# A batched float32 matrix product on one core: moving the transposes of the last three batches from the batch before into their own batch

## The chip, the cores and the metric

The kernel runs on one core of a Trainium2 chip. The metric is device time in microseconds (us) of one execution. Medians of several executions are given. Two numbers must be kept apart: the device time of a run, and the span of its profile, which goes from the first to the last instruction of the kernel and is 1.7 to 1.9 us shorter. Profiles show one execution each, so times that are read inside a profile are compared with an anchor inside the same profile.

## The reference

```python
def setup_inputs():
    batch, m, k, n = 32, 512, 1024, 768
    # x: [32, 512, 1024] float32, weight: [32, 1024, 768] float32, random normal

def reference(x, weight):
    return np.matmul(x, weight).astype(np.float32)
```

## The kernel before

Each batch loads x (2 MiB of float32 in HBM, the chip's main memory) and the weight (3 MiB), both cast to bfloat16 on the way by GpSimd's DMA queue, and stores 1.5 MiB of float32. (Only x of batch 0 is loaded otherwise: by SP, as float32.) TensorE (PE) must have x transposed, so it also does transposes: four of them make one row tile `xT` of 128 rows, which VectorE copies out of PSUM, the memory that PE writes to. A batch has four row tiles `mt`; two of them make a pair, whose results are copied out by ScalarE and VectorE (`evacuate`).

The last four batches (`CHUNKED`) take their weight in pieces along the contraction, so that PE can start before the whole weight is there. All other loads and the stores of outputs 0 to 30 are issued by GpSimd; the two halves of output 31 are issued by SP (SyncE), on another DMA queue.

```python
    CHUNKED = {B - 4: (4, 4), B - 3: (4, 4), B - 2: (4, 4), B - 1: (4, 2, 2)}
    AHEAD = 3
    # ... (pools, loads)
    def transpose(b, mt):
        pt = tpsum.tile([P, JT, P], F32, name="pt")
        pairs = xs[b].bitcast(F32)
        for j in range(JT):
            nc.tensor.transpose(pt[:, j, :], pairs[:, mt, j::JT], ident)
        xT = xT_pool.tile([P, JT, P, 2], BF16, name="xT")
        nc.vector.tensor_copy(...)          # cut
        return xT
    # ... (first batch, matmuls)
    def evacuate(b, pair, pm):
        o = outs[b][:, pair * N2:(pair + 1) * N2]
        nc.scalar.copy(o[:, 0:512], pm[0])
        nc.vector.tensor_copy(o[:, 512:1024], pm[1])
        nc.scalar.copy(o[:, 1024:N2], pm[2])
    # ...
        ready = {}
        for b in range(B):
            if b + AHEAD < B:
                load_x(b + AHEAD)
                load_w(b + AHEAD)
            if b > 0:
                nc.gpsimd.dma_start(out=out_view[b - 1], in_=outs[b - 1])
            outs[b] = out_pool.tile([P, MT * N], F32, name="out_sb")
            if b not in CHUNKED:
                # ... (cut: batches 0 to 27, untouched by the change)
                continue
            xT = ready.pop(b, None) or {mt: transpose(b, mt) for mt in range(MT)}
            pms = [banks() for _ in range(2)]
            at = 0
            for n in CHUNKED[b]:
                last = at + n == KT
                for mt in range(MT):
                    if last and b + 1 < B:
                        ready.setdefault(b + 1, {})[mt] = transpose(b + 1, mt)
                    matmuls(pms[mt // 2], mt % 2, xT[mt], b, range(at, at + n), True)
                    if last and mt % 2 == 1:
                        pair = mt // 2
                        evacuate(b, pair, pms[pair])
                        if b == B - 1:
                            cols = slice(pair * N2, (pair + 1) * N2)
                            nc.sync.dma_start(out_view[b, :, cols], outs[b][:, cols])
                at += n
```

## Time and profile before

| | before |
|---|---|
| device time, median of 3 | 516.92 us (516.58 to 517.77) |
| span of the profile | 516.0 us |
| PE / VectorE / ScalarE busy | 83% / 25% / 15% |
| x 31 landed, last half of output 31 landed | 489.1 us, 514.8 us |

From the page of the kernel before: the DMA queue table (packets, MB, share of the sixteen DMA engines' span) and the summary of the chain of waits by engine.

```profile
q0 software_dynamic: 14256, 131.60, 98.9%
q1 hardware_dynamic: 432, 3.67, 1.9%
...
DMA 88%; PE 9%; issue 1%; DVE 0%; ACT 0%; POOLq 0%
```

Queue 0 (GpSimd's) keeps the sixteen DMA engines busy for 98.9% of the span, and the chain of waits is nearly all DMA. The kernel is bound by DMA, at a fixed beat: 1.5 MiB (counted as float32) land every 3.66 us.

The timeline of the kernel before, some lines of its tail (start, duration, engine, line, operation, and in brackets the idle time before it and what ended it):

```profile
479.18 6.66 PE L99 MATMUL pm<-w_sb,xT 128*128 128x256 bf16 x39
...
489.12 0.75 PE L68 MATMUL pt<-ident,x_sb 128*128 128x128 f32 x4 [3.28 <-DMA x_sb<-in_x_dram]
...
496.67 11.86 PE L99 MATMUL pm<-w_sb,xT 128*128 128x256 bf16 x71
...
499.19 0.53 POOL L130 DMA_DIRECT2D out_dram<-out_sb  x1 [16.95 <-ACT out_sb L112]
...
507.89 1.62 SPq L159 DMA_DIRECT2D out_dram<-out_sb  x2
```

PE stops at about 485.8 us and waits for x 31, with half of batch 30 still to do, because the transposes of 31 stand before that half. So output 30 is issued by GpSimd only at 499.19, and output 31 by SP at 507.89 (and 509.2).

How long those stores took, from the list of DMA issues in the tail of the kernel before (KB each, median us from issue to landing):

```profile
out_dram<-out_sb POOLq DMA_DIRECT2D x1, 1536.0 KB, 11.9
out_dram<-out_sb SPq DMA_DIRECT2D x2, 768.0 KB, 5.3
```

Output 30 landed at 499.19 + 11.9 = 511.1 us. Issue plus time to landing gives every landing in this text; below they are given to a hundredth, from the semaphore events of the trace.

The DMA engines over the tail of the kernel before, in stretches of 2 us (the last two columns are the busy share of the sixteen engines and GB/s):

```profile
core 0: us, PE busy (x) PEld busy (x) DVE busy (x) ACT busy (x) POOL busy (x), PEclk, DMA share, GB/s
503.00:505.00 2.00, 1.95 (x13) 1.13 (x12) 0.00 (x0) 0.00 (x0) 0.00 (x0) 1.00 0.97 412
505.00:507.00 2.00, 2.00 (x14) 1.27 (x13) 0.00 (x0) 0.44 (x1) 0.00 (x0) 1.00 0.75 320
507.00:509.00 2.00, 1.53 (x10) 0.68 (x7) 1.33 (x2) 1.70 (x4) 0.00 (x0) 1.00 0.45 187
509.00:511.00 2.00, 0.00 (x0) 0.00 (x0) 0.05 (x1) 0.16 (x1) 0.00 (x0) 1.00 1.01 415
511.00:513.00 2.00, 0.00 (x0) 0.00 (x0) 0.00 (x0) 0.00 (x0) 0.00 (x0) 1.00 0.80 326
```

The dip at 505 to 509 us looks like time that an earlier output 31 could fill.

### The profile page before, as it was taken

What the parts mean: (1) busy time and instruction counts of PE and PEld (TensorE: products, weight loads), DVE (VectorE), ACT (ScalarE), POOL (GpSimd) and SP (SyncE); (2) the same over time, 40 slices, a digit from 0 to 9 for tenths busy, and PEclk for the clock granted to TensorE, in tenths of its full rate; (3) what the DMA queues carried; (4) which work ended last, traced back from release to release, by engine and by line L of the source; (5) the groups of instructions that cost most, each with busy time, mean ns of one, the idle gap of its engine ahead of it and who ended that gap; (6) DMA issues with size and microseconds to landing.
All of it is one profiled execution on the core that took longest, in us unless ns stands there. A gap on an engine that the chain in (4) does not pass through costs nothing.

```text
span 516.0 us, 5924 instructions
## 1 busy us (share of the span) xinstructions
PE 426.4 (83%) x2528; PEld 279.6 (54%) x2576; DVE 129.7 (25%) x196; ACT 76.3 (15%) x129; POOL 53.4 (10%) x105
## 2 busy tenths in 40 slices
PE   0999998698887879977798797987878987969794
PEld 0766665465554555654555464654545554646462
DVE  0433333133131231322313232222223132312221
ACT  0111111011111111110111011111111110101111
POOL 3011010100101001100011001010100110111000
PEclk9999999799898997998989799898989898979989
DMA  8999999999999999999999999999999999999996
GB/s 255 218 218 211 215 274 275 272 272 241 255 280 273 275 254 241 276 277 274 267 240 268 274 276 272 247 252 278 275 274 256 247 267 275 276 267 239 259 390 261
DMA packets 14714, 135.65 MB, mean 263 GB/s; under 512 B 1632, under 2 KB 1632, under 8 KB 3040
## 3 DMA queue, kind: packets, MB, share of 16 engines
q0 software_dynamic: 14256, 131.60, 98.9%
q1 hardware_dynamic: 432, 3.67, 1.9%
q8 instruction: 20, 0.33, 0.2%
q14 instruction: 6, 0.05, 0.0%
HBM read 167.77 MB, written 50.33 MB: 423 GB/s over the span
## 4 chain that ended last, share of the span: by engine, by line
DMA 88%; PE 9%; issue 1%; DVE 0%; ACT 0%; POOLq 0%
DMA x_sb<-in_x_dram 37%; DMA w_sb<-in_weight_dram 25%; DMA out_dram<-out_sb 24%; PE pm L99 7%; DMA x_first<-in_x_dram 2%; PE pt L81 1%; PE pt L68 1%; DVE out_sb L111 0%; DVE xT L70 0%; ACT out_sb L112 0%; POOLq L130 0%; POOLq L54 0%; POOLq L60 0%
## 5 line engine op out<-in xcount | busy, mean ns | idle before, releaser
L99 PE MATMUL pm<-w_sb,xT 128*128 128x256 bf16 (+1 forms) x2000 | 370.2, 340 | 60.9 <-DMA w_sb<-in_weight_dram 56.8
L99 PEld LDWEIGHTS <-xT 128*128 128x128 bf16 x2048 | 206.8, 102 | 198.3 <-issue 66.5
L70 DVE COPY xT<-pt 128x1024 bf16<-128x1024 bf16 x124 | 83.0, 689 | 245.4 <-PE pt L68 245.4
L68 PE MATMUL pt<-ident,x_sb 128*128 128x128 f32 x496 | 77.4, 290 | 8.9 <-DMA x_sb<-in_x_dram 8.6
L68 PEld LDWEIGHTS pt<-ident,x_sb 128*128 128x128 f32 x496 | 73.7, 207 | 17.2 <-issue 7.1
L110 ACT COPY out_sb<-pm 128x512 f32<-128x512 f32 x64 | 37.5, 586 | 289.6 <-PE pm L99 280.7
L111 DVE COPY out_sb<-pm 128x512 f32<-128x512 f32 x64 | 43.9, 687 | 115.5 <-PE pm L99 114.8
L112 ACT COPY out_sb<-pm 128x512 f32<-128x512 f32 x64 | 37.5, 586 | 142.5 <-PE pm L99 142.4
L54 POOL DMA_DIRECT2D x_sb<-in_x_dram x31 | 16.5, 533 | 172.8 <-DMA w_sb<-in_weight_dram 141.6
L60 POOL DMA_DIRECT2D w_sb<-in_weight_dram x37 | 19.8, 534 | 132.4 <-DMA out_dram<-out_sb 65.6
L130 POOL DMA_DIRECT2D out_dram<-out_sb x31 | 16.6, 536 | 140.8 <-DMA x_sb<-in_x_dram 62.8
L81 PE MATMUL pt<-ident,x_first 128*128 128x128 f32 x32 | 5.7, 338 | 12.4 <-DMA x_first<-in_x_dram 12.4
L81 PEld LDWEIGHTS pt<-ident,x_first 128*128 128x128 f32 x32 | 4.9, 202 | 13.0 <-issue 12.3
L82 DVE CAST xT<-pt 128x512 bf16<-128x512 f32 x8 | 5.5, 727 | 18.4 <-PE pt L81 18.3
L110 ACT ACT_TABLE_LOAD x1 | 1.3, 1283 | 0.7 <-PEq L175 0.7
masks.py:199 POOL TENSOR_SCALAR_AFFINE_SELECT ident<-ident 128x128 f32<-128x128 f32 x1 | 0.3, 288 | 0.1
masks.py:197 POOL MEMSET ident<- 128x128 f32 x1 | 0.2, 223 | 0.0
L175 POOL MEMSET const-float32-0.0<- 128x1 f32 x1 | 0.1, 99 | 0.2 <-issue 0.2
L175 POOL MEMSET const-bfloat16-1.0<- 128x1 bf16 x1 | 0.1, 102 | 0.0
L175 POOL MEMSET const-uint8-127<- 128x1 uint8 x1 | 0.1, 102 | 0.0
L175 POOL MEMSET const-float32-1.0<- 128x1 f32 x1 | 0.1, 98 | 0.0
## 6 DMA issues: line engine op xcount, KB each, us to landing
out_dram<-out_sb POOLq DMA_DIRECT2D x31, 1536.0 KB, 41.9
w_sb<-in_weight_dram POOLq DMA_DIRECT2D x28, 1536.0 KB, 43.2
x_sb<-in_x_dram POOLq DMA_DIRECT2D x31, 1024.0 KB, 39.6
w_sb<-in_weight_dram POOLq DMA_DIRECT2D x7, 768.0 KB, 32.5
x_first<-in_x_dram SPq DMA_DIRECT2D x1, 2048.0 KB, 11.5
out_dram<-out_sb SPq DMA_DIRECT2D x2, 768.0 KB, 5.3
w_sb<-in_weight_dram POOLq DMA_DIRECT2D x2, 384.0 KB, 28.7
```

Source lines behind the costliest of these rows:

```text
L54: nc.gpsimd.dma_start(out=xs[b], in_=x_view[b])
L60: nc.gpsimd.dma_start(out=ws[b][:, at:at + n, :], in_=w_view[b, :, at:at + n, :])
L68: nc.tensor.transpose(pt[:, j, :], pairs[:, mt, j::JT], ident)
L70: nc.vector.tensor_copy(xT.rearrange("p j m r -> p (j m r)"), pt.bitcast(BF16).rearrange("p j m -> p (j m)"))
L81: nc.tensor.transpose(pt[:, i, :], x_first[:, mt, JT * h + i::KT], ident)
L82: nc.vector.tensor_copy(xT[:, 2 * h:2 * h + 2].rearrange("p j m r -> p j r m"), pt.rearrange("p (j r) m -> p j r m", r=2),)
L99: nc.tensor.matmul(pm[bank][:, at:at + size], xT[:, ko // 2, :, ko % 2], ws[b][:, ko, off:off + size], start=(ko == 0 and not (together an ...
L110: nc.scalar.copy(o[:, 0:512], pm[0])
L111: nc.vector.tensor_copy(o[:, 512:1024], pm[1])
L112: nc.scalar.copy(o[:, 1024:N2], pm[2])
L130: nc.gpsimd.dma_start(out=out_view[b - 1], in_=outs[b - 1])
L175: nc = _bacc.Bacc("TRN2", target_bir_lowering=False, num_devices=1)
```

## The change

The intent: a batch's transposes should not stand in the way of the batch before. In the last four batches they are issued in the batch's own first chunk, each one tile ahead of its matmuls. (Batch 28 did its own transposes before the change too, all four ahead of its matmuls; for batches 29 to 31 they move.) Nothing is added or removed; only PE's order changes.

```diff
-        ready = {}
         for b in range(B):
@@
-            xT = ready.pop(b, None) or {mt: transpose(b, mt) for mt in range(MT)}
+            xT = {0: transpose(b, 0)}
@@
                 for mt in range(MT):
-                    if last and b + 1 < B:
-                        ready.setdefault(b + 1, {})[mt] = transpose(b + 1, mt)
+                    if mt + 1 not in xT and mt + 1 < MT:
+                        xT[mt + 1] = transpose(b, mt + 1)
                     matmuls(pms[mt // 2], mt % 2, xT[mt], b, range(at, at + n), True)
```

## The prediction

> **What bounds the kernel.** The DMA. The queue table gives queue 0 (GpSimd's) 98.9% of the sixteen engines' span; the chain of waits is 88% DMA, 9% PE. Landings (issue plus time to landing) come at a fixed beat: 1.5 MiB of float32 per 3.66 us (an output, or half a weight, counted at float32), 4.86 us for the 2 MiB of an x. That is 430 GB/s; the Trainium skill ("DMA: Bandwidth & Descriptors", Specifications) gives 435 GB/s as the fabric ceiling, and this trace sits on it. 208 MiB at that beat take 507.5 us of the 516.0 us span (estimate).
>
> **What the change does.** Nothing is added or removed: transposes, matmuls, copies, DMAs and the order of GpSimd's issues stay. Only PE's order in the last four batches changes. Before, the second half of batch b stood behind the transposes of b+1, so behind x of b+1: the timeline shows PE restarting at 457.5, 473.3 and 489.1 us, when x 29, 30 and 31 land, with half of the batch before still to do. After, batch b needs only its own x and w.
>
> Costs: four transposes about 0.65 us, their copy 0.69 us, half a batch of matmuls 5.1 to 5.4 us warm. With w halves landing at 461.0/464.7, 476.9/480.6 and, for batch 31, 492.7/494.6/496.5, I estimate PE's end of batch 29 at 470 instead of 479, of 30 at 486 instead of 497, of 31 at 504 to 506 instead of 508.6. Batch 31 keeps a cold start (granted clock 0.57 in 490 to 494 before): PE idles before x 31 and before w 31. Output 30 is then issued about 487 instead of 499.2, output 31 from 504 instead of 507.9.
>
> **How much is critical.** Nearly nothing. The tail looks like a loss: the DMA share falls to 0.60, 0.43, 0.46 in 506 to 509 us, 1.6 us missing. But landings show no gap: outputs 27 to 30 at 500.1, 503.8, 507.5, 511.1, the halves of 31 at 513.0 and 514.8, all on the beat (1.85 for a half). I read this as sixteen engines finishing their backlogs unevenly: the fast ones run dry at 505.5 us, the slowest works without pause to the end. An output has landed when its slowest engine is done, so output 31 queued earlier fills only idle engines. Both queues share the same engines (same page, "Issuing engines are not separate DMA queues"); the slowest has the same bytes to move. Output 30 was already queued 8 us before its turn, the second half of 31 about 2 us.
>
> **Predicted time:** 516.8 us, 516.0 to 517.8 (three runs before spread over 1.2 us). Faster by over 2%: 0.005; within 2%: 0.99; slower: 0.005.
>
> **What would show each step.** Right: PE no longer waits for x 29, 30, 31 with old work behind it; last matmul at 503 to 507 us; output 31 issued some 3 us earlier; more DMA share in 505 to 509, less in 509 to 513; yet the last landing near 514.8, x 31 near 489, same beat. Wrong: a last landing near 513, so the dip was a true loss.
>
> **What would make it wrong.** The slowest engine did wait for output 31 (at most 1.6 us: 515.2). Or w 31 or the cold clock push the last matmul past 510 (about +1). Or interleaving the queues longer changes its beat. Stray pauses of 0.5 to 1 us (landings at 250.9, 445.2) come and go and are as large as any effect here.

## More of the kernel before

The next lines were there before the prediction too, but I did not look at them. They are instructions of the kernel's closing sequence, which all stand under one line (L186, `with _tile.TileContext(nc) as tc:`): the view of that source line gives the count, the shortest, median and longest duration in ns, and the start of the first and the last.

```profile
L186 POOLq EVENT_SEMAPHORE  x4: 17/17/17, 515.2 to 515.9; - x4
L186 POOLq DRAIN  x3: 46/102/16031, 499.2 to 515.7; - x3
L186 SPq DRAIN  x3: 7/7/7, 514.9 to 515.5; - x3
```

GpSimd's DRAIN begins at 499.17 us, together with its issue of output 30 (499.19), and this one instruction takes 16.03 us: it ends at 515.20 us. SP, which waits for the last landing (514.80), is through at 514.94. So the end of the program waited for GpSimd's drain, by 0.26 us, and not for the last landing.

## The result, and the profile after

| | before | after |
|---|---|---|
| device time, median (range), 6 runs each | 516.88 us (516.58 to 517.77) | 518.25 us (517.45 to 519.31) |
| ratio | | 1.0025 (95%: 1.0011 to 1.0039) |

A ratio is the mean time of one kernel's fast runs over that of the other's of the same rounds, so it is not quite the ratio of the medians. The change costs about 1.3 us. That is within 2%, but outside noise and outside the predicted range (516.0 to 517.8).

The profile of after has a span of 517.5 us. The same timeline lines, of after:

```profile
482.39 7.96 PE L99 MATMUL pm<-w_sb,xT 128*128 128x512 bf16 x48
...
490.19 1.12 PE L68 MATMUL pt<-ident,x_sb 128*128 128x128 f32 x8
...
491.41 0.53 POOL L129 DMA_DIRECT2D out_dram<-out_sb  x1 [9.33 <-ACT out_sb L112]
...
498.48 7.96 PE L99 MATMUL pm<-w_sb,xT 128*128 128x512 bf16 x48
...
505.80 1.62 SPq L158 DMA_DIRECT2D out_dram<-out_sb  x2
```

PE did what was intended: batch 30 is finished before PE turns to x 31, output 30 is issued 7.8 us earlier and output 31 2.1 us earlier. The stores of after, from its list of DMA issues:

```profile
out_dram<-out_sb POOLq DMA_DIRECT2D x1, 1536.0 KB, 21.3
out_dram<-out_sb SPq DMA_DIRECT2D x2, 768.0 KB, 7.8
```

Output 30, though issued earlier, landed later: 491.41 + 21.3 = 512.7 us. The DMA engines over the tail of after:

```profile
core 0: us, PE busy (x) PEld busy (x) DVE busy (x) ACT busy (x) POOL busy (x), PEclk, DMA share, GB/s
503.00:505.00 2.00, 2.00 (x15) 1.22 (x14) 0.00 (x0) 0.54 (x1) 0.00 (x0) 1.00 1.01 430
505.00:507.00 2.00, 1.44 (x9) 0.67 (x7) 1.38 (x2) 1.70 (x4) 0.00 (x0) 1.00 0.86 363
507.00:509.00 2.00, 0.00 (x0) 0.00 (x0) 0.00 (x0) 0.06 (x1) 0.00 (x0) 1.00 1.00 418
509.00:511.00 2.00, 0.00 (x0) 0.00 (x0) 0.00 (x0) 0.00 (x0) 0.00 (x0) 1.00 0.89 372
511.00:513.00 2.00, 0.00 (x0) 0.00 (x0) 0.00 (x0) 0.00 (x0) 0.00 (x0) 0.53 0.49 206
```

The dip is filled, and the bytes are missing later. The closing sequence of after (its line is L185):

```profile
L185 POOLq EVENT_SEMAPHORE  x4: 17/17/17, 516.8 to 517.4; - x4
L185 POOLq DRAIN  x3: 46/102/25367, 491.4 to 517.2; - x3
L185 SPq DRAIN  x3: 7/7/7, 515.3 to 517.0; - x3
```

GpSimd's drain starts at 491.39, takes 25.37 us and ends at 516.76. SP had been through at 515.36 and waited 1.4 us for it. Set beside the landings, the two profiles agree to a hundredth:

| us | before | after |
|---|---|---|
| x 31 landed | 489.08 | 489.49 |
| output 29 landed | 507.45 | 507.87 |
| output 30 landed | 511.11 | 512.67 |
| last half of output 31 landed | 514.80 | 515.22 |
| ... counted from x 31 | 25.72 | 25.73 |
| GpSimd's drain ended | 515.20 | 516.76 |
| ... counted from output 30's landing | 4.09 | 4.09 |
| end of span, counted from the drain's end | 0.76 | 0.76 |

Of the 1.56 us between the two spans, 0.41 us were already there when x 31 landed (it landed between 487.9 and 489.5 us in the thirteen traces, whatever the kernel), and the rest, 1.15 us, is the later landing of output 30.

### The profile page after: what moved, and what is told of

Its sections match the earlier page's. It is cut to its first block, busy times and chain, and to the rows that moved or that the text cites. A ratio compares the mean times of both kernels' runs of the same rounds, so it can differ in the third digit from the quotient of the medians.

```text
span 517.5 us, 5978 instructions
## 1 busy us (share of the span) xinstructions
PE 428.0 (83%) x2576; PEld 278.9 (54%) x2576; DVE 129.8 (25%) x196; ACT 76.2 (15%) x129; POOL 53.3 (10%) x105
## 4 chain that ended last, share of the span: by engine, by line
DMA 81%; PE 15%; issue 1%; DVE 1%; ACT 0%; POOLq 0%
DMA w_sb<-in_weight_dram 47%; DMA out_dram<-out_sb 25%; PE pm L99 12%; DMA x_sb<-in_x_dram 8%; DMA x_first<-in_x_dram 2%; PE pt L68 1%; PE pt L81 1%; DVE xT L70 1%; DVE out_sb L111 0%; ACT out_sb L112 0%; POOLq L60 0%; POOLq L54 0%
## 5 line engine op out<-in xcount | busy, mean ns | idle before, releaser
L68 PE MATMUL pt<-ident,x_sb 128*128 128x128 f32 x496 | 75.5, 286 | 1.1 <-DMA x_sb<-in_x_dram 1.1
## 6 DMA issues: line engine op xcount, KB each, us to landing
w_sb<-in_weight_dram POOLq DMA_DIRECT2D x2, 384.0 KB, 28.7
```

## The theories

**Tail theory.** The end of the program waits for GpSimd's closing drain, and the drain ends 4.09 us after GpSimd's own last store, output 30, has landed. Output 31 is on the other queue. Queued earlier, its packets take turns with those of output 30 on the slowest DMA engine; the sum of bytes is the same, so the last landing does not move, but output 30 lands later, and with it the end of the drain. The Trainium skill ("DMA: Bandwidth & Descriptors", section "Queues, rings and completion order") says that each DMA engine goes round the queue rows that have work for it, a packet at a time. The sizes of the delays in these traces agree with that (below, under the table of all tails).

**Rivals.** PE: its new order, its idle times or its clock cost the time (in the profile of after the granted clock, the share of its full clock that PE was given, was 0.57 in 494 to 498 us). Noise: the 0.41 us and their like, pauses in the DMA beat that come and go.

## The experiments

Runs of one group were on the same chip and share the runs of the kernel before.

### First group: the changed kernel again, its halves, and a needless delay

**after_again**: the changed kernel, no edit.

> The changed kernel as it is, once more, for a second trace and a closer interval. Tail theory (GpSimd's last drain returns about 4.1 us after its last own store, output 30, has landed, and output 31, queued earlier on the other DMA queue, takes turns with output 30 on the slowest DMA engine): 1.0 to 1.6 us slower than before; output 30 lands 1.0 to 1.4 us later than 3.66 us after output 29; the drain ends 4.1 us after that landing; output 31 still lands 25.7 us after x 31. Rival, noise and stray pauses early in the run: within 0.4 us of before, or slower with x 31 landing later by as much. Rival, PE: the last matmul would be later than before's 508.5 us.

Measured: 518.39 us against 517.01, ratio 1.0025 (1.0013 to 1.0037). In its trace output 31 was issued at 502.7, even earlier: this time PE had the full clock in batch 31 (granted 1.00 from 486 to 498 us; last matmul at 503.3). It had the low one before, in batch 30 (0.61 and 0.54 in 474 to 482 us). Output 30 landed 5.50 us after output 29, so 1.84 us late, and the drain ended 4.09 us after that. The last landing came 25.76 us after x 31. The delay of output 30 was larger than the 1.0 to 1.4 us expected. The rest held. So the loss is repeatable, it is there without a cold clock in batch 31 (and in only31_own, below, with a clock of 1.00 in every stretch from 470 to 502 us), and it is there with PE ending 4 us earlier than in the kernel before (503.3 against 507.4 in before_again below, whose x 31 landed at the same 488.0 us).

**only31_own** and **own_but31**: half of the change each. A set `OWN` names the batches that transpose for themselves; the others are served a batch ahead as before. It holds `(B - 1,)` in the first and `(B - 4, B - 3, B - 2)` in the second.

```diff
-            xT = ready.pop(b, None) or {mt: transpose(b, mt) for mt in range(MT)}
+            xT = {0: transpose(b, 0)} if b in OWN else ready.pop(b, None) or {mt: transpose(b, mt) for mt in range(MT)}
@@
-                    if last and b + 1 < B:
+                    if mt + 1 not in xT and mt + 1 < MT:
+                        xT[mt + 1] = transpose(b, mt + 1)
+                    if last and b + 1 < B and b + 1 not in OWN:
```

> Only batch 31 is changed: its transposes are among its own matmuls; 29 and 30 are still transposed a batch ahead. Tail theory: all of the loss is here, 1.0 to 1.6 us slower than before, output 31 issued near 506 and 507 us, output 30 late by over 0.8 us against the beat. Rival, that the loss comes from PE's idle times and cold clock in all of the batches 28 to 31: a part of it, about a third.

> The complement: batches 28 to 30 are changed, 31 is still transposed a batch ahead, among the last matmuls of 30. Tail theory: level with before within 0.4 us, since output 31 is issued near 508 and 509 us as before and output 30 lands on the beat. Rival, that the loss comes from PE's idle times and cold clock in the batches 28 to 31: about two thirds of the loss, 0.8 us slower than before.

Measured: batch 31 alone 518.50 us, ratio 1.0028 (1.0016 to 1.0041); batches 28 to 30 alone 517.00 us, ratio 0.9999 (0.9987 to 1.0011), both against 517.01. The whole loss comes with batch 31 and none with the other three. Output 31 was issued at 502.9 us in the first (expected: near 506) and at 507.0 in the second. The drains, from the view of the closing line of each kernel, first of batch 31 alone:

```profile
L189 POOLq DRAIN  x3: 46/93/24967, 491.2 to 516.7; - x3
```

and of batches 28 to 30 alone:

```profile
L189 POOLq DRAIN  x3: 46/93/16022, 498.2 to 514.8; - x3
```

The first ends at 491.24 + 24.97 = 516.21 us, the second at 498.25 + 16.02 = 514.27 us. Output 30 was 1.83 us late against the beat in the first and 0.03 us in the second.

**after_late_store**: the changed kernel, with four needless copies on ScalarE that hold output 31 back. The result is the same.

```diff
                     if last and mt % 2 == 1:
                         pair = mt // 2
+                        if b == B - 1 and pair == 0:
+                            for _ in range(4):
+                                nc.scalar.copy(outs[b][:, 0:512], pms[0][0])
                         evacuate(b, pair, pms[pair])
```

> The changed kernel with four needless copies of the first PSUM bank on ScalarE ahead of the last batch's copies, so that both stores of output 31 are issued about 2.3 us later, where the kernel before has them. Same result, same values. Tail theory: output 30 lands on the beat again (3.66 to 4.0 us after output 29), the drain ends earlier, and the kernel is 0.8 to 1.4 us faster than the changed kernel, level with before within 0.4 us, although its last store is issued later. Any rival in which the end waits for the last store or for PE: no faster than the changed kernel, up to 2 us slower.

Measured: 517.27 us, ratio 1.0000 (0.9987 to 1.0012) against before, 1.1 us faster than the changed kernel of the same rounds (518.39). Added work and a later last store (504.8 and 505.8 us, against 502.7 and 504.0 in after_again, the trace of the same rounds) made the kernel faster. This is what the tail theory says and what no theory allows in which the end waits for PE or for the last store. One number was off: output 31 was issued at 504.8 us, still 1.5 us before output 29 had landed, so output 30 was 0.67 us late, not on the beat.

### Second group: which queue the last stores are on

**before_pool_store** and **after_pool_store**: output 31 is issued by GpSimd, behind output 30 in the same queue. One edit, made in both kernels:

```diff
-                            nc.sync.dma_start(out_view[b, :, cols], outs[b][:, cols])
+                            nc.gpsimd.dma_start(out_view[b, :, cols], outs[b][:, cols])
```

> The kernel before with the two stores of output 31 issued by GpSimd, not by SP, so that they stand in GpSimd's own queue behind output 30. Tail theory: output 31 lands at about the same time after x 31 (25.7 us, up to 0.5 more), the drain ends 4.1 us after that, so the span ends about 4.9 us after the last landing and not 1.2: 3 to 4.5 us slower than before. Rival (the end follows the last landing whatever the queue): within 0.7 us of before.

> The changed kernel with the same edit. With one queue there are no turns to take: outputs 30 and 31 land on the beat, one after the other. Tail theory: 3 to 4.5 us slower than before, and level with the kernel before that has the same edit, within 0.5 us; the loss by the change is gone, although PE's order differs as before. Rival, that PE's order costs the time: again 1.0 to 1.6 us slower than the kernel before with this edit.

Measured: 521.12 us and 520.69 us against 517.09, both with ratio 1.0074 (1.0062 to 1.0086). The loss by the change is gone once there is only one queue, although PE's order still differs (last matmul at 507.8 and at 503.6 us). Output 30 landed 3.71 and 3.65 us after output 29, on the beat, even with output 31 queued at 503.4. And both pay about 3.8 us, because now the drain follows the last store of all. The drain of the kernel before with this edit:

```profile
L186 POOLq DRAIN  x3: 46/87/9450, 508.8 to 518.8; - x3
```

It ends at 508.85 + 9.45 = 518.30 us, 4.17 us after the last half of output 31 (514.13). In the changed kernel with this edit it ends 4.17 us after the same landing as well (514.02, 518.19).

**before_sp30** and **after_sp30**: output 30 is taken from GpSimd and issued by SP between the two halves of output 31. Again one edit in both:

```diff
-            if b > 0:
+            if 0 < b < B - 1:
                 nc.gpsimd.dma_start(out=out_view[b - 1], in_=outs[b - 1])
@@
                             nc.sync.dma_start(out_view[b, :, cols], outs[b][:, cols])
+                            if pair == 0:
+                                nc.sync.dma_start(out_view[b - 1], outs[b - 1])
```

> The kernel before with output 30 taken from GpSimd's queue and issued by SP between the two halves of output 31. GpSimd's last store is output 29, so its drain ends near 511.6 us and off the critical path; the end follows the last landing by about 1.2 us. But the slowest DMA engine has nothing left from about 505.7 us until output 31 is issued at 507.9[...]. Tail theory: that engine idles for 2.5 to 3 us, and the kernel is 2 to 3 us slower than before. Rival, that the last landing does not depend on PE's end: level with before.

> The changed kernel with the same edit. Output 31's first half is issued at 505.8 us, just when the slowest engine runs dry. Tail theory: GpSimd's drain ends near 512 us, the slowest engine pauses for no more than 0.6 us, the span ends about 1.2 us after the last landing: 0.6 to 1.4 us faster than the changed kernel, within 0.5 us of before, and 2 to 3 us faster than the kernel before with this edit; here PE's earlier end is worth what it saves. Rival, that the loss is PE's: still 1.0 to 1.6 us slower than before.

Measured, against 517.09: the kernel before with this edit 518.19 us, ratio 1.0015 (1.0000 to 1.0029), with a wide spread (516.74 to 519.34); the changed kernel with this edit 516.42 us, ratio 0.9988 (0.9976 to 1.0000). Now the changed kernel is the faster one of the pair, by 1.8 us of the medians (about 1.4 us by the two ratios). That is less than the 2 to 3 us expected.

The drain is off the critical path in both: it ends at 510.57 and 510.40 us, 4.05 us after output 29. What decides is whether the DMA engines run dry before output 31 comes. The kernel before with this edit:

```profile
core 0: us, PE busy (x) PEld busy (x) DVE busy (x) ACT busy (x) POOL busy (x), PEclk, DMA share, GB/s
503.00:505.00 2.00, 2.00 (x14) 1.18 (x13) 0.00 (x0) 0.00 (x0) 0.00 (x0) 1.00 0.36 154
505.00:507.00 2.00, 2.00 (x15) 1.26 (x13) 0.69 (x1) 1.23 (x3) 0.00 (x0) 1.00 0.06 25
507.00:509.00 2.00, 0.62 (x4) 0.12 (x2) 0.69 (x1) 1.07 (x2) 0.00 (x0) 1.00 0.60 246
```

and the changed kernel with this edit:

```profile
core 0: us, PE busy (x) PEld busy (x) DVE busy (x) ACT busy (x) POOL busy (x), PEclk, DMA share, GB/s
503.00:505.00 2.00, 0.26 (x2) 0.00 (x0) 0.69 (x1) 0.71 (x2) 0.00 (x0) 1.00 0.89 372
505.00:507.00 2.00, 0.00 (x0) 0.00 (x0) 0.00 (x0) 0.00 (x0) 0.00 (x0) 0.84 1.09 458
507.00:509.00 2.00, 0.00 (x0) 0.00 (x0) 0.00 (x0) 0.00 (x0) 0.00 (x0) 0.50 0.96 406
```

Where the engines ran dry, the last landing came 27.68 us after x 31; where they did not, 25.78. In the seven traces of the table below it was 25.72 to 25.77, so the slowest engine had not paused in them, as the prediction read it. The pause cost 1.9 us of landing, less than the 2.5 to 3 us expected, and 1.1 us of the median, less than the 2 to 3 us expected.

### Third group: noise, and a version for the end

**before_again**: the kernel before against itself.

> The kernel before against itself, for a second trace of it and for the size of the noise. Ratio 1.000 within 0.0015. GpSimd's drain ends 4.09 us after output 30 has landed, the span 0.75 us after the drain; output 30 lands within 0.1 us of the 3.66 us beat after output 29.

Measured: 517.50 us against 516.99, ratio 1.0006 (0.9994 to 1.0018). The drain ended 4.09 us after output 30, which landed exactly on the beat. So a ratio of 1.0006 between runs of one kernel is noise, and 1.0025 twice is not.

**after_sp30_again**: no further edit.

> The changed kernel with output 30 issued by SP between the halves of output 31, once more, for a closer interval against before. 0.3 to 1.2 us faster than before (ratio 0.998 to 0.9995); the span ends 0.9 us after the last landing, which comes 25.8 us after x 31.

Measured: 516.69 us against 516.99, ratio 0.9995 (0.9982 to 1.0008). With the first time (0.9988), this version is 0.3 to 0.7 us of the medians below the kernel before, but the second interval includes no difference. It beats the changed kernel clearly, and the kernel before at best by a hair.

**after_sp30_k15**: a gamble on the slowest DMA engine.

```diff
-                            nc.sync.dma_start(out_view[b, :, cols], outs[b][:, cols])
+                            for rows in (slice(0, 120), slice(120, P)):
+                                nc.sync.dma_start(out_view[b, rows, cols], outs[b][rows, cols])
```

(and the same for output 30).

> The same, with the three stores of SP each cut into 120 and 8 partitions, a gamble on which DMA engine is the slowest. If a store of 120 partitions goes to fifteen of the engines and the one it leaves out is the slowest, the last landing comes 1 us earlier after x 31 (about 24.7 us) and the kernel is about 1 us faster than the uncut one. If another engine is the slowest, that one gets more to do: 0.2 to 0.8 us slower than the uncut one.

Measured: 521.05 us, ratio 1.0087 (1.0066 to 1.0109), 4.4 us slower than the uncut version of the same rounds. In its tail the DMA share was 0.95, 0.96 and 0.99 in the three stretches of 2 us from 505 to 511, which does not tell whether the cut left an engine out. The last landing came 28.7 us after x 31, 3 us later than uncut. The gamble is lost, by more than either branch of the expectation allowed, and it does not tell which engine is the slowest.

### All tails side by side

"Lead" is how long before output 29's landing SP issued the first half of output 31. "Late" is how much output 30's landing missed the beat of 3.66 us after output 29.

| kernel | lead | output 30 late | last landing from x 31 | end of span from x 31 | median |
|---|---|---|---|---|---|
| before | -0.44 | 0.00 | 25.72 | 26.88 | 516.88 |
| before_again | -0.40 | 0.00 | 25.77 | 26.92 | 517.50 |
| own_but31 | -0.48 | 0.03 | 25.75 | 26.92 | 517.00 |
| after_late_store | 1.48 | 0.67 | 25.77 | 27.60 | 517.27 |
| after | 2.07 | 1.14 | 25.73 | 28.03 | 518.25 |
| after_again | 3.69 | 1.84 | 25.76 | 28.76 | 518.39 |
| only31_own | 3.71 | 1.83 | 25.75 | 28.73 | 518.50 |

The landing of the last half (fourth column) is constant. The end of the span (fifth) grows with the lateness of output 30 (third), one for one. The lateness is about half of the lead (second) in the four traces that have one.

The list of DMA packets in the packed traces tests the turn-taking more closely. GpSimd's queue moves output 30 in 128 packets of 12,288 bytes; SP's moves each half of output 31 in 128 packets of 6,144. If both are spread evenly over the sixteen engines (not shown), an engine has 8 packets of each, and one of SP's takes about 0.23 us (an estimate: the second half lands 1.83 us after the first in the kernel before). The delays 0.67, 1.14 and 1.84 us are then nearly whole numbers of SP's packets, 3, 5 and 8: as if one went in between for each packet of output 30 that was still to come. The turns do not begin with the issue, though: SP's first packet started 0.84 us after it in the trace of after, but 2.4 us after it (505.10 us) in that of after_again. Why stays open.

## Why the prediction was wrong

- **What bounds the kernel, and what the change does to PE: right, but for batch 30.** The last matmul came at 506.4 us (predicted 503 to 507), output 31 was issued at 505.8 (predicted from 504; in the second trace 502.7). But PE ended batch 30 at 490.35 us (482.39 + 7.96), not 486, so it had no idle time before x 31 (489.5), and output 30 was issued at 491.4, not 487. The fabric ceiling of 435 GB/s (the Trainium skill, "DMA: Bandwidth & Descriptors", Specifications) to which the prediction compares the beat (430 GB/s, counted as float32) is close to it in size; but while x lands, half as many bytes after the cast, the trace counts only 208 to 210 GB/s at the same beat (470 to 474 and 486 to 490 us), so it is not shown that this ceiling sets the beat.
- **"The slowest works without pause to the end", "the last landing near 514.8": right.** The last landing came 25.73 us after x 31, and 25.72 before. before_sp30 showed what a real pause does to that number (27.68). That the engines finish unevenly can be seen too: in the packed trace each store has sixteen completion events, as many as there are engines, and those of output 29 came from 502.26 to 507.45 us before; where the queue had run dry (before_sp30), those of the next store came within 0.2 us. More DMA share in 505 to 509 and less later: right, 0.75 and 0.45 became 0.86 and 1.00.
- **The step that failed: "An output has landed when its slowest engine is done, so output 31 queued earlier fills only idle engines", and the silent step after it, that the time ends with the last landing.** On the slowest engine output 31 did not find idle time; it took turns with output 30 and put it back by 1.14 us (1.84 in the second trace). The prediction counted the sum of bytes of that engine, which stayed, and not their order, which changed. And the order matters because the end of the span follows the drain that waits for GpSimd's last store: 4.09 us after output 30, in each of the seven traces of the table above. That term, +1.15 us of the span in the profile and +1.4 us of the median, was missing from the sum.
- It was to be had from the trace before. The drain of 16.03 us was there, and it already ended 0.26 us after SP was through. The chain of waits did not show it: its last link is ScalarE's last copy at 508.6 us, and what comes after that is not on it.
- **The other dangers named** were not the cause. Neither w 31 nor the cold clock pushed the last matmul past 510 us (506.4 and 503.3), and in these two traces the loss was smaller with the cold clock (output 30 late by 1.14 us) than without (1.84), where output 31 came earlier. "Interleaving the queues longer changes its beat" came nearest: the beat stayed, but the order of landings within it changed.

That turn-taking is the mechanism is inferred, from four observations: output 30 was late only when two queues had work, on the beat with the same early issue in one queue, the later the greater the lead, and by nearly whole numbers of SP's packets. Which of the sixteen engines is the slowest, and why, stays open; the traces do not name a packet's engine. What GpSimd does in the 4.09 us stays open too.

## What to carry to other kernels

When a kernel is bound by DMA, look past the last landing: read what each engine does in the closing sequence, and which DMA it waits for. Put the very last stores on a queue whose issuer does not need long to close, and do not let them overtake a store that the slow closer waits for. An engine that finishes earlier is worth something only if what it releases does not get in the way of what ends last: here the same change cost 1.4 us of the medians with one order of stores and saved 1.8 us with another.

## What the Trainium skill lacked or had wrong

- No page gives the time that GpSimd's closing drain takes after its last store: 4.09 us after the landing in seven traces, 4.17 us where the last stores were the two halves of output 31, 4.05 us where it was output 29. It belongs to "DMA: Bandwidth & Descriptors", beside the fixed cost of a GpSimd DMA.
- "VectorE: DVE Perf Modes", section "The DRAIN you can't avoid", tells of two kinds of DRAIN: the flush after an operation of VectorE, and the runtime's boilerplate of about 12 ns on all five engines. The drains here fit neither: they stand under a line of the program (L186, the TileContext's), and while SP's took 7 ns, the longest of GpSimd's took 16,031 ns before and 25,367 ns after, and it set the end of the program. No page tells of these.
- "DMA: Bandwidth & Descriptors", section "Issuing engines are not separate DMA queues", says that issuing DMAs from several engines saves only the sequencer's issue time. Here the choice of the issuing engine moved the time by about 3.8 us (ratio 1.0074), with the same bytes to move, through the drain; and with two queues in place of one the change cost 1.3 us (ratio 1.0025), put down above to the turns that they take.
